# An RWKV-7 recurrence on one core: where a unit's first score pair stands, which queue carries three of its transfers, and when v is added

## The chip, the core and the metric

The kernel runs on one core of a Trainium2 chip. The core has a matrix engine (TensorE, "PE" in the profile), a vector engine (VectorE, "DVE"), a scalar engine (ScalarE, "ACT"), a general engine (GpSimd, "POOL") and a queue-only engine (SyncE, "SP"). Each has its own instruction stream, and they meet through semaphores. Sixteen DMA engines move data between DRAM and on-chip memory; here SyncE, ScalarE and GpSimd issue DMAs. An issue that waits for a semaphore holds up everything behind it on its engine. The metric is the device time of one execution in microseconds.

## The reference

One step of a trunk of two layers, for a prompt of 2048 tokens (with 16 learned tokens ahead of it) and for 8 samples of 4 tokens. Layer 0 is sliding-window attention. Layer 1 is RWKV-7 time mixing, with 16 heads of 64; its core, per token and head, is

```
sa = jnp.einsum('bhvk,bhk->bhv', S, a_t)
S = S * w_t[:, :, None, :] + sa[..., None] * b_t[:, :, None, :] + v_t[..., None] * k_t[:, :, None, :]
y_t = jnp.einsum('bhvk,bhk->bhv', S, r_t)
...
y = ((y - mean) * lax.rsqrt(var + GN_EPS)).reshape(B, T, R_WIDTH)
y = y * ln_g.astype(f32) + ln_b.astype(f32)
bonus = jnp.sum(r_h * k_h * r_k.astype(f32), axis=-1, keepdims=True) * v_h
y = (y + bonus.reshape(B, T, R_WIDTH)) * jax.nn.silu(g.astype(f32))
out = jnp.einsum('btw,wd->btd', y.astype(xn.dtype), w_out)
```

Then `out` is added to the residual, and a last RMS norm gives the result. The outputs are the normed rows, the attention windows, the last states S and the last rows of both layers' inputs.

## The kernel before

The program has three stages: attention (to about 600 us of the profiled span), the projections of the RWKV layer (to about 1600), and the recurrence (to the end). The change touches the third alone.

**Units and chunks.** The recurrence works on units of 128 tokens; unit 0 holds the learned tokens, units 1 to 16 the prompt, and the samples come last. A unit has four chunks of 32 tokens, counted from 0 here; where the text says third or fourth chunk, that is chunk 2 or 3. Within a chunk the per-token recurrence is replaced by matrix products: the 32 updates form a triangular system with one matrix per head. Its inverse depends on keys and decays alone, not on the state, and is prepared one or two units ahead. With it a chunk is this chain, in `chain` (line 1422) and `solve` (1394):

1. TensorE: `C<-Z,L`, the right-hand side from the state; ScalarE copies it to `R0s`. Z holds the state (64 rows) above the chunk's 32 rows of v and the 32 of the solution.
2. TensorE: `C<-R0s,TT`, the solve with the inverted triangles TT; ScalarE copies the result into Z (`Z<-C`, four copies).
3. TensorE: `C<-Z,LS`, the new state; VectorE scales it into the next chunk's Z (`Z<-C,pe`).

DMAs bring the rows of v for the next chunk into its Z (`Z<-v`, `new_Z`, `load_v`, lines 1359 to 1372), two a chunk. At the ends of chunks 1 and 3 (counted from 0) TensorE also makes the outputs `Y<-Z,L`.

**Work between the steps.** Other products of TensorE fill the time in which a chunk's chain waits for the other engines: the output projection of the unit before (`po<-wo,yp`), the gate (`pd<-wg,xg`, multiplied in by VectorE as `gt<-gt,pd`), transposes (`yps`), keys (`kt`), and the scores. A score pair is the scores of two chunks of the unit two ahead, `pz<-L,BK`, 64 matmuls in the profile (32 as the program writes them; `scores`, line 948). ScalarE copies the triangles out of them (`LAs<-pz`, four copies), VectorE masks the rest (`L<-pz,smk`, four products). BK and L come by DMA.

**The inverse** (`inverse`, line 976). When both pairs are there, LAs goes to DRAM (`la_d<-LAs`, two DMAs) and comes back with another layout (`LA<-la_d`, two DMAs). GpSimd scales it (`LA<-LA,ln`), then inverts by rows, in a chain of some 31 pairs `XT<-LA,X` and `X<-X,XT`, and scales the result (`X<-X,ln`). It goes to DRAM (`tt_d<-X`) and back as TT (`TT<-tt_d`), which the next unit's first solve needs. GpSimd also does small steps of two norms (`var`, `ms`) in the midst of that chain.

**After Y.** `group_norm` (1583) subtracts means, scales by `var`, by gamma (`lng`), adds beta (`lnb`), and at last v times the bonus (`ytm<-ytm,vt`, two products on VectorE). The gate multiplies it, TensorE transposes it, and `project_out` (1685) gives the residual's new rows, which leave by `out_y_prompt<-h`.

**What sets the order.** For units 2 to 14, `steady` (1766) writes the work out by hand, chunk by chunk, and `in_order()` (1753) fixes the order of VectorE, ScalarE and GpSimd as it is written; parts inside `released()` are free of that. TensorE's fillers are cut to budgets (`run(pe[ch], 1.2)`). The other units and SyncE's queue are ordered by a scheduler with priorities, so that a DMA's place on SyncE's queue can move when other things move. The helpers `mm`, `act`, `tt`, `stt` and `dma` record all operations on lines 38 to 50, so the profile's rows are told apart by their names.

In `steady`, `s` is the unit two ahead. Before the change the two score pairs are made in chunks 1 and 2, ahead of the solve, and `inverse(s)` begins in chunk 3:

```
if ch == 1:
    new_LAs(s)
if ch == 2:
    outputs(u, 1)
if ch in (1, 2):
    sc = scores(s, ch - 1)
    next(sc)
```

Of the kernel before, what the change touches and what calls it, by code (L numbers as in the profile page):

```python
# [30 lines left out]
def tile_hybrid_step(ctx: ExitStack, tc: tile.TileContext, a, o, c):  # L31
# [17 lines left out]
    def dma(out, in_, eng=None):  # L49
        return (eng or nc.sync).dma_start(out=out, in_=in_).ins  # L50
# [925 lines left out]
    def inverse(u, room=None, ln=None):  # L976

        nch = u.nch
        nl = nch * 16
        la_d = dramr.tile([2, nl // 2, 32, 32], F32, name="la_d", tag=f"la_d{nch}")  # L980
        u.tt_d = tt_d = dramr.tile([32, 4, 4 * nch * 32], F32, name="tt_d", tag=f"tt_d{nch}")
        for e in range(2):
            dma(la_d[e].rearrange("l j i -> j l i"),
                u.LAs[32 * e:32 * e + 32].rearrange("p h c g i -> p (h c g) i"), s_ if u.idx < PRE else None)
        eng = v_ if u.idx == 1 else g_
        if u.kind == "m":
            room = wl.tile([P, 2, 32 * 32], F32, name="roomm", tag="L", bufs=nbuf["L"])
        if room is not None:
            LA = room[:, 0].rearrange("p (j i) -> p j i", i=32)
            XX = room[:, 1].rearrange("p (a k i) -> p a k i", a=2, i=32)  # L990
        else:

            LA = wk.tile([P, 32, 32], F32, name="LA", tag="LA", bufs=2)
            XX = None
        if XX is None:
            X = wk.tile([P, 16, 32], F32, name="X", tag="X", bufs=2)
            XT = wk.tile([P, 16, 32], F32, name="XT", tag="XT")
        else:
            X, XT = XX[:, 0], XX[:, 1]
        if ln is None:  # L1000
            ln = wp.tile([P, 32], F32, name="ln", tag=("mu", "rst0")[u.idx % 2])
        if nch < 4:
            g_.memset(LA, 0.0)
            g_.memset(ln, 1.0)
        for hh in range(2):
            dma(LA[hh * 64:hh * 64 + nl], la_d.rearrange("e l j i -> (e l) j i"), s_ if u.idx < PRE else None)
            dma(ln[hh * 64:hh * 64 + nl], ln_d[u.idx].rearrange("q c g i -> (q c g) i"))
        tt(eng, LA, LA, ln.unsqueeze(2).broadcast_to([P, 32, 32]), ALU.mult)
        dma(X, c["laneid"])

        low = 16 if u.kind == "m" else 0

        part = {2: 16}.get(u.idx, 0)
        cut = [(v_, 0, part), (g_, part, 16)] if 0 < part < 16 else [(v_, 0, 16)] if part else [(eng, 0, 16)]
        for j in range(low, 31):
            if j in (8, 16, 22, 26):
                yield
            w = 3 - j % 4 if u.kind == "s" else 31 - j
            for eng, k0, k1 in cut if w else ():
                ks = slice(max(low // 2, k0), min(j // 2 + 1, k1))  # L1020
                shape = [P, ks.stop - ks.start, w]
                if shape[1] <= 0:
                    continue
                tt(eng, XT[:, ks, :w], LA[:, j:j + 1, j + 1:j + 1 + w].broadcast_to(shape), X[:, ks, j:j + 1].broadcast_to(shape), ALU.mult)
                tt(eng, X[:, ks, j + 1:j + 1 + w], X[:, ks, j + 1:j + 1 + w], XT[:, ks, :w], ALU.add)
        for eng, k0, k1 in reversed(cut):
            u.inverted = tt(eng, X[:, k0:k1], X[:, k0:k1], ln[:, None, :].broadcast_to([P, k1 - k0, 32]), ALU.mult)
        for hh in range(2):
            dma(tt_d[hh:32:2].rearrange("k q (l i) -> (q l) k i", i=32), X[hh * 64:hh * 64 + nl])
# [238 lines left out]
    with ExitStack() as ph:  # L1268
# [62 lines left out]
        def new_LAs(u):  # L1331
            u.LAs = wk.tile([64, 2, u.nch, 4, 32], F32, name="LAs", tag="LAs", bufs=1)
# [23 lines left out]
        anchors = {}  # L1356
        MARK = -1

        def new_Z(u, ch):

            Z = Zs[Zcount[0] % nbuf["Z"]]
            Zcount[0] += 1
            for e in range(2):
                load_v(u, ch, e, Z)
            return Z

        def load_v(u, ch, e, Z):
            b0, r0 = OS[e].start, u.off + ch * 32
            anchors["SP"] = dma(Z[b0 + 32:b0 + 64, e].rearrange("p g d -> p (g d)"), v_d[u.t][r0:r0 + 32, e, :])

        LScount = [0]
        over = []
# [32 lines left out]
        def released():  # L1405

            st = ExitStack()
            for x in anchors.values():
                st.enter_context(tc.issue_after(x))
            return st  # L1410
# [11 lines left out]
        def chain(u, ch):  # L1422
# [15 lines left out]
            anchors["PE"] = m  # L1438
            anchors["ACT"] = act(R0s, C[0][:, 0])

            if ch + 1 < u.nch:
                Zn = new_Z(u, ch + 1)
                u.Z.append(Zn)
            elif u.next is not None:
                Zn = new_Z(u.next, 0)
                u.next.Z.append(Zn)
            else:
                Zn = None
# [317 lines left out]
        def steady(i, u, pe):  # L1766
# [9 lines left out]
            for ch in range(4):  # L1776
# [4 lines left out]

                left = rests[::-1]
                del rests[:]
                with released():
                    if ch == 2:
                        next(inv.get(i + 1, idle()), None)
                for gen in left:
                    run(gen, to=MARK)
                with released():
                    for fn in side:  # L1790
                        fn()
                    del side[:]
                    if ch == 1:
                        new_LAs(s)
                    if ch == 2:
                        outputs(u, 1)
                    if ch in (1, 2):
                        sc = scores(s, ch - 1)
                        next(sc)
                    if ch == 3:  # L1800
                        kt = keys(u.next, 0)
                        next(kt)
# [4 lines left out]
                else:  # L1807
                    for gen in left:
                        run(gen)
                if ch in (1, 2):  # L1810
                    with released():
                        all_of(sc)
                run(pe[ch], 1.2)
                next(rec)
                with released():
                    if ch == 0:
                        kt = keys(u, 1) if i > 2 else idle()
                        next(kt, None)
                        first = L0s.pop(s.idx, None)
                        load_BK(s)  # L1820
                        s.L.append(first or load_L(s, 0))
                        all_of(kt)
                    if ch == 3:
                        all_of(kt)
                        inv[s.idx] = inverse(s)
                        next(inv[s.idx])
                    else:
                        next(inv.get(i + 1, idle()), None)
                if ch < 3:
                    run(norm, to=MARK)  # L1830
                else:
                    run(norms_[u.idx], to=MARK)
                run(pe[ch], 1.9)
                next(rec, None)
# [11 lines left out]
                run(pe[ch], to=MARK)  # L1846
                if ch == 0:
                    run(norm, to=MARK)
                rests.append(pe[ch])
                for part in PLAN.get((i, ch), ()):  # L1850
                    with released():
# [214 lines left out]
```

## Time and profile before

| what | value |
|---|---|
| time, median of 3 runs | 2562.52 us (2557.93 to 2570.88) |
| the profiled execution | 2564.59 us, its span 2562.7 us |
| mean granted TensorE clock | 0.945 |
| busy: TensorE, VectorE | 2245.7 us (88%), 1681.5 us (66%) |
| busy: ScalarE, GpSimd | 1168.8 us (46%), 1041.8 us (41%) |
| DMA | 312.99 MB, mean 122 GB/s |
| the recurrence's 13 hand-ordered units | from 1709.4 to 2359.1 us |

The page gives each engine's busy time, the chain that ended last, and groups of instructions with their idle time ahead. In a row of a timeline the numbers are the start and the length in microseconds, then engine, line, operation and tiles; brackets hold the idle time ahead and what ended it. "PE pz L38 <- DMA BK<-bk" in the waits means that TensorE's pz matmuls waited for that DMA. A DMA's row on SyncE ("SPq") shows its issue, not its transfer. In the chain of waits a DMA's row runs from the issue to the landing. The busy share of TensorE is an average over three stages; for this change only the rows from about 1640 us on matter.

### The profile page before, as it was taken

Reading aid. Unit: us, or ns where it says so; the run is one execution under the profiler, and the core shown is the slowest. Engines: PE = TensorE matmul, PEld = TensorE weight load, DVE = VectorE, ACT = ScalarE, POOL = GpSimd, SP = SyncE. Lnnn points to the kernel's source line nnn. Section 1 sums busy time; section 2 is a strip of 40 time slices with the busy share of each in tenths; the row PEclk is TensorE's granted clock in tenths of the full one; section 3 lists DMA queues with packets and bytes.
Section 4 is the critical chain, followed back from the end, with each engine's and each line's share of the span. In section 5 each row is a group of like instructions: output and inputs, shape, how many; then the busy total and the mean of one; then the engine's idle time right before and its main releaser. Section 6 shows DMA issues by size and latency. Waiting matters only on the chain.

```text
span 2562.7 us, 60891 instructions
## 1 busy us (share of the span) xinstructions
PE 2245.7 (88%) x24932; PEld 1544.6 (60%) x24932; DVE 1681.5 (66%) x3181; ACT 1168.8 (46%) x2799; POOL 1041.8 (41%) x1572
## 2 busy tenths in 40 slices
PE   6999999899999897899999998657887887888897
PEld 5877777777845445576677766344554554454553
DVE  7586674667747987766665556465666666666674
ACT  6676455566523344454444345233453444344432
POOL 4242122322111444433332333244667656666613
PEclk9999998999999998999999999768998999898998
DMA  8433222332447564322222225474555556455423
GB/s 205 124 108 111 68 67 79 132 99 74 139 114 234 198 232 147 121 84 103 78 93 89 92 86 164 102 219 110 137 135 130 122 135 144 103 137 131 106 62 74
DMA packets 346235, 312.99 MB, mean 122 GB/s; under 512 B 205546, under 2 KB 282218, under 8 KB 344131
## 3 DMA queue, kind: packets, MB, share of 16 engines
q1 hardware_dynamic: 337171, 296.71, 40.0%
q10 hardware_dynamic: 7168, 8.59, 1.6%
q0 software_dynamic: 1616, 3.79, 0.7%
q8 instruction: 196, 3.21, 0.5%
q14 instruction: 84, 0.69, 0.1%
HBM read 191.15 MB, written 119.84 MB: 121 GB/s over the span
## 4 chain that ended last, share of the span: by engine, by line
PE 33%; DVE 19%; DMA 17%; POOL 10%; ACT 9%; issue 8%; SPq 4%; ACTq 0%; POOLq 0%; DVEq 0%
PE pd L38 19%; PE po L38 5%; DVE xm L47 5%; SPq L50 4%; DMA BK<-bk 3%; DMA TT<-tt_d 3%; POOL X L44 3%; PE C L38 2%; DVE xpr L44 2%; POOL XT L44 2%; ACT ssb L41 2%; DMA wst<-in_rwkv_w_in 2%; DMA tt_d<-X 1%; PE pz L38 1%; DMA x<-in_x_prompt 1%
## 5 line engine op out<-in xcount | busy, mean ns | idle before, releaser
L38 PEld LDWEIGHTS <-yp 128*128 128x128 f16 x1488 | 143.2, 101 | 173.4 <-issue 25.7
L47 DVE SCALAR_TENSOR_TENSOR xm<-dx,mu,xn 128x256 f32<-128x256 f32 (+2 forms) x432 | 200.2, 522 | 48.1 <-POOL dx L44 47.3
L44 POOL TENSOR_TENSOR X<-X,XT 128x126 f32<-128x126 f32 (+24 forms) x458 | 196.9, 430 | 35.7
L38 PE MATMUL po<-wo,yp 128*128 128x512 f16 x768 | 201.5, 408 | 0.0
L38 PE MATMUL pd<-xp,wq 128*128 128x256 f16 (+2 forms) x1728 | 184.7, 265 | 12.3 <-DVE qp L47 9.0
L38 PE MATMUL pd<-wg,xg 128*128 128x512 f16 (+1 forms) x816 | 194.0, 385 | 0.5 <-issue 0.3
L44 POOL TENSOR_TENSOR XT<-LA,X 128x126 f32<-128x126 f32 (+24 forms) x458 | 175.8, 384 | 40.4 <-issue 6.7
L38 PE MATMUL pd<-wvv,xpr 128*128 128x512 f16 (+1 forms) x816 | 188.5, 388 | 0.0
L38 PE MATMUL pd<-xp,wg 128*128 128x256 f16 (+2 forms) x1728 | 186.6, 270 | 0.9 <-DVE xp L44 0.5
L38 PE MATMUL pd<-xpr,w 128*128 128x256 f16 (+2 forms) x1728 | 185.6, 267 | 0.0
L38 PE MATMUL pd<-xpr,wkk 128*128 128x256 f16 (+2 forms) x1728 | 179.5, 264 | 0.0
L38 PEld LDWEIGHTS <-wq 128*128 128x128 f16 x1728 | 158.5, 98 | 33.3 <-DVE qp L47 10.5
L44 POOL TENSOR_TENSOR ssb<-ssb,bias 128x512 f32<-128x512 f32 x64 | 86.3, 1355 | 222.8 <-DVE ssb L462 179.0
L38 PEld LDWEIGHTS <-wg 128*128 128x128 f16 x1728 | 161.4, 100 | 23.6 <-issue 4.0
L38 PEld LDWEIGHTS <-w 128*128 128x128 f16 x1728 | 157.3, 99 | 26.8 <-issue 9.7
L38 PEld LDWEIGHTS <-wkk 128*128 128x128 f16 x1728 | 158.2, 98 | 15.6 <-issue 0.4
L38 PE MATMUL pd<-w,yp 128*128 128x512 f16 x720 | 161.6, 382 | 4.2 <-DMA yp<-y 4.2
L44 POOL TENSOR_TENSOR ps<-wst,ps 128x1024 f16<-128x1024 f32 x32 | 69.5, 2171 | 221.8 <-ACT wst L41 203.7
L44 DVE TENSOR_TENSOR Z<-C,pe 64x256 f32<-64x256 f32 x256 | 108.0, 422 | 68.4 <-PE C L38 53.0
L38 PEld LDWEIGHTS <-xpr 128*128 128x128 f16 (+1 forms) x816 | 79.1, 100 | 102.1 <-issue 17.6
L44 DVE TENSOR_TENSOR xpr<-xm,xpr 128x512 f16<-128x512 f32 (+2 forms) x144 | 98.9, 708 | 55.2 <-ACT xpr L41 54.8
L41 ACT ACTIVATE ssb<-ssb,ng 128x128 f32<-128x128 f32 (+1 forms) x272 | 104.2, 384 | 57.0 <-DVE es L44 53.4
(357 smaller groups left out, 4699.1 us busy)
## 6 DMA issues: line engine op xcount, KB each, us to landing
wst<-in_rwkv_w_in SPq DMA_DIRECT2D x32, 512.0 KB
wsp<-ps SPq DMA_DIRECT2D x32, 512.0 KB
BK<-bk SPq DMA_DIRECT2D x32, 512.0 KB
x<-in_x_prompt SPq DMA_DIRECT2D x29, 512.0 KB
xn<-xn SPq DMA_DIRECT2D x14, 1028.0 KB
ar<-aro SPq DMA_DIRECT2D x28, 512.0 KB
bk<-bko SPq DMA_DIRECT2D x28, 512.0 KB
L<-ar SPq DMA_DIRECT2D x38, 256.0 KB
```

The costliest lines, as they stand in the source:

```text
L38: return t_.matmul(out=out, lhsT=lhsT, rhs=rhs, start=start, stop=stop, **kw).ins
L41: return s_.activation(out=out, in_=in_, func=func, **kw).ins
L44: return e.tensor_tensor(out=out, in0=in0, in1=in1, op=op).ins
L47: v_.scalar_tensor_tensor(out=out, in0=in0, scalar=scalar, in1=in1, op0=op0, op1=op1)
L50: return (eng or nc.sync).dma_start(out=out, in_=in_).ins
```

## The change

Four things change in the recurrence, for the hand-ordered units.

- **Scores.** The first pair of the unit two ahead is made at the end of chunk 1, behind that chunk's state update, no longer at its head. The second stays in chunk 2.
- **Triangles' way out.** `la_d<-LAs` is issued by ScalarE (before: SyncE, but for the first units), in chunk 2, directly behind the copies that fill LAs. The function `inverse` gets a `yield` there, so that the loads back, `LA<-la_d`, are still placed in chunk 3.
- **Rows of v.** For all but the first and last units the `Z<-v` loads are issued by ScalarE, behind its copy to `R0s`.
- **v added.** The last part of the group norm, `ytm<-ytm,vt`, runs at the head of chunk 3, no longer in chunk 2.

The diff, without hunk lines:

```diff
 def inverse(u, room=None, ln=None):
...
             dma(la_d[e].rearrange("l j i -> j l i"),
-                u.LAs[32 * e:32 * e + 32].rearrange("p h c g i -> p (h c g) i"), s_ if u.idx < PRE else None)
+                u.LAs[32 * e:32 * e + 32].rearrange("p h c g i -> p (h c g) i"), s_)
+        yield
         eng = v_ if u.idx == 1 else g_
...
-        def new_Z(u, ch):
+        def new_Z(u, ch, eng=None):
...
-                load_v(u, ch, e, Z)
+                load_v(u, ch, e, Z, eng)
...
-        def load_v(u, ch, e, Z):
+        def load_v(u, ch, e, Z, eng=None):
             b0, r0 = OS[e].start, u.off + ch * 32
-            anchors["SP"] = dma(Z[b0 + 32:b0 + 64, e].rearrange("p g d -> p (g d)"), v_d[u.t][r0:r0 + 32, e, :])
+            x = dma(Z[b0 + 32:b0 + 64, e].rearrange("p g d -> p (g d)"), v_d[u.t][r0:r0 + 32, e, :], eng)
+            if eng is None:
+                anchors["SP"] = x
...
             anchors["ACT"] = act(R0s, C[0][:, 0])

+            eng = s_ if 1 < u.idx < len(us) - 2 else None
             if ch + 1 < u.nch:
-                Zn = new_Z(u, ch + 1)
+                Zn = new_Z(u, ch + 1, eng)
                 u.Z.append(Zn)
             elif u.next is not None:
-                Zn = new_Z(u.next, 0)
+                Zn = new_Z(u.next, 0, eng)
...
         def steady(i, u, pe):
...
                 left = rests[::-1]
                 del rests[:]
+                if ch == 3:
+                    run(norm)
                 with released():
                     if ch == 2:
                         next(inv.get(i + 1, idle()), None)
...
-                    if ch == 1:
-                        new_LAs(s)
                     if ch == 2:
                         outputs(u, 1)
-                    if ch in (1, 2):
-                        sc = scores(s, ch - 1)
+                        sc = scores(s, 1)
                         next(sc)
...
-                if ch in (1, 2):
+                if ch == 2:
                     with released():
+                        inv[s.idx] = inverse(s)
+                        next(inv[s.idx])
                         all_of(sc)
                 run(pe[ch], 1.2)
                 next(rec)
...
                     if ch == 3:
                         all_of(kt)
-                        inv[s.idx] = inverse(s)
                         next(inv[s.idx])
...
-                if ch < 3:
+                if ch < 2:
                     run(norm, to=MARK)
-                else:
+                elif ch == 3:
                     run(norms_[u.idx], to=MARK)
...
                 if ch == 0:
                     run(norm, to=MARK)
+                if ch == 1:
+                    with released():
+                        new_LAs(s)
+                        all_of(scores(s, 0))
                 rests.append(pe[ch])
```

The diff shows little of what happens to the queues. Three places do.

First SyncE's queue, in a unit in the middle of the recurrence (v_110 and the like are buffers of one block), from one `out_y_prompt` toward the next. Before:

```order
L50 DMA xg<-xg_130 128x16x128
L50 DMA BK<-bk_150 128x4x256 x2
...
L50 DMA ln<-ln_192 64x32 x2
L50 DMA X<-c_laneid 128x512
L50 DMA Z_19046<-v_111 32x512
L50 DMA la_d<-LAs 32x32x32 x2
L50 DMA L<-ar_159 64x1024
L50 DMA tt_d<-X 64x16x32 x2
L50 DMA LA<-la_d 64x1024
L50 DMA vt<-v_110 128x512 x2
L50 DMA LA<-la_d 64x1024
L50 DMA TT<-tt_d 64x1x512 x2
```

and now:

```order
L50 DMA xg<-xg_130 128x16x128
L50 DMA BK<-bk_150 128x4x256 x2
L50 DMA bont<-bo_211 128x16
L50 DMA L<-ar_159 64x1024 x2
L50 DMA tt_d<-X 64x16x32 x2
L50 DMA ln<-ln_193 64x32 x2
L50 DMA LA<-la_d 64x1024 x2
L50 DMA TT<-tt_d 64x1x512 x2
L50 DMA X<-c_laneid 128x512
L50 DMA vt<-v_110 128x512 x2
L50 DMA out_y_prompt<-h_25545 128x1024
```

la_d and the rows of v are gone from it, vt stands behind TT and no longer between the two LA, and ln and X<-c_laneid, which belong to a later inverse, stand behind tt_d.

Second, ScalarE from the state copy of chunk 1 to that of chunk 2 in the same part of the program. Before:

```order
L41 ACTIVATE R0s<-C 128x256
L41 ACTIVATE po,ssq_24848<-h_24847 128x512
L41 ACTIVATE LAs<-pz 32x2x128 x4
L41 ACTIVATE Z_19046<-C 32x256 x4
...
L41 ACTIVATE LAs<-pz 32x2x128 x4
L41 ACTIVATE Z_19047<-C 32x256 x4
```

and now:

```order
L41 ACTIVATE R0s<-C 128x256
L50 DMA Z_19047<-v_109 32x512 x2
L41 ACTIVATE po,ssq_24848<-h_24847 128x512
L41 ACTIVATE Z_19046<-C 32x256 x4
L41 ACTIVATE LAs<-pz 32x2x128 x4
...
L50 DMA Z_19044<-v_109 32x512 x2
...
L41 ACTIVATE LAs<-pz 32x2x128 x4
L50 DMA la_d<-LAs 32x32x32 x2
L41 ACTIVATE Z_19047<-C 32x256 x4
```

The first LAs copies moved behind chunk 1's Z copies; the rows of v and la_d are new, la_d ahead of chunk 2's Z copies. On TensorE, in chunk 2, the second score pair stood ahead of the whole solve and now stands in its middle, behind VectorE's masks of the first pair:

```order
L38 MATMUL C<-R0s,TT 32x64 x8
L38 MATMUL pz<-L,BK 64x64 x32
L38 MATMUL C<-R0s,TT 32x64 x8
```

Third, SyncE's queue at the start of the recurrence, where the blocks of the output weights (wo) are loaded; the tt_d and TT shown are those of unit 2, the first of the hand-ordered ones. Before:

```order
L50 DMA wo_20144<-wsp_225 128x2048
L50 DMA wo_20146<-wsp_226 128x2048
L50 DMA tt_d<-X 64x16x32 x2
L50 DMA TT<-tt_d 64x1x512 x2
```

and now:

```order
L50 DMA wo_20144<-wsp_225 128x2048
L50 DMA wo_20146<-wsp_226 128x2048
L50 DMA wo_20255<-wsp_227 128x2048
L50 DMA wo_20257<-wsp_228 128x2048
L50 DMA xg<-xg_126 128x16x128
L50 DMA tt_d<-X 64x16x32 x2
L50 DMA wo_20437<-wsp_229 128x2048
L50 DMA wo_20439<-wsp_230 128x2048
...
L50 DMA wo_20590<-wsp_232 128x2048
L50 DMA h_20659<-h_1_84 128x1024
...
L50 DMA TT<-tt_d 64x1x512 x2
```

All eight blocks of wo, and a residual's rows, now stand ahead of that TT on the queue; before, six of them stood behind it.

## The prediction, made before the changed kernel ran

> **What bounds the kernel now.** I first read which waits stop TensorE in the nine units from 1860 to 2311 us, where each unit of 128 tokens repeats the last (us in total, times, longest):
>
> ```profile
> PE pz L38 <- DMA BK<-bk: 42.0, 13, 5.5
> PE C L38 <- DMA TT<-tt_d: 13.3, 10, 2.2
> PE C L38 <- issue: 11.9, 8, 1.5
> ```
>
> The large wait, 4.7 us a unit, is on BK, the operand of the score matmuls. It would be easy to stop here and credit the change with it. But TT, GpSimd's inverted triangles, is waited for in every unit as well, so TensorE would only reach the next TT sooner. I therefore read GpSimd's groups over the same stretch, and its timeline around one inverse:
>
> ```profile
> L44 POOL TENSOR_TENSOR LA<-LA,ln 128x1024 f32<-128x1024 f32 x10 | 19.1, 1915 | 104.6 <-DMA LA<-la_d 63.9 <-DMA bont<-bo 20.7 <-DMA out_y_prompt<-h 10.9
> ```
> ```profile
> 1765.56 0.56 POOL L44 TENSOR_TENSOR XT<-LA,X 128x31 f32<-128x31 f32 x1
> ...
> 2161.13 0.24 POOL L44 TENSOR_TENSOR XT<-LA,X 128x31 f32<-128x31 f32 x1
> ...
> 2197.46 1.65 POOL L44 TENSOR_TENSOR X<-X,ln 128x512 f32<-128x512 f32 x1
> 2209.72 1.92 POOL L44 TENSOR_TENSOR LA<-LA,ln 128x1024 f32<-128x1024 f32 x1 [10.62 <-DMA bont<-bo]
> 2211.72 0.24 POOL L44 TENSOR_TENSOR XT<-LA,X 128x31 f32<-128x31 f32 x1
> ...
> 2312.62 0.56 POOL L44 TENSOR_TENSOR XT<-LA,X 128x31 f32<-128x31 f32 x1
> ```
>
> GpSimd stands idle 10.46 us (104.6 over 10) ahead of every inverse and is otherwise in its chain of XT and X products. The first and last XT rows shown are 547.06 us and 11 inverses apart: 49.73 us each. One inverse, from 2161.13 to the end of its last product at 2199.11, is 38.0 us; then come 12.6 us to the next XT. A period is that inverse plus that gap. GpSimd sets the pace as well as TensorE, and the question is what fills the gap. The rows of SyncE's queue answer it:
>
> ```profile
> 2197.83 0.97 SPq L50 DMA_DIRECT2D la_d<-LAs  x2
> 2198.86 0.63 SPq L50 DMA_DIRECT2D L<-ar  x1
> 2199.57 1.34 SPq L50 DMA_DIRECT2D tt_d<-X  x2
> 2201.02 1.06 SPq L50 DMA_DIRECT2D LA<-la_d  x1
> 2202.18 1.02 SPq L50 DMA_DIRECT2D vt<-v  x2
> 2203.25 0.48 SPq L50 DMA_DIRECT2D LA<-la_d  x1
> 2203.82 1.10 SPq L50 DMA_DIRECT2D TT<-tt_d  x2
> ...
> 2207.34 0.38 SPq L50 DMA_DIRECT2D out_y_prompt<-h  x1
> ```
>
> The inverse ends at 2199.11. The scores go out to DRAM (la_d) only 1.3 us before that, the second half of LA is issued at 2203.25 behind 512 KB of vt, and its consumer starts 6.0 us after that issue ends. TT is last.
>
> **The change part by part.** The period is worked out for two loops; the slower one counts.
>
> GpSimd's loop. la_d now leaves ScalarE's queue in the third chunk, so it has landed before the inverse under way ends. vt goes behind TT. What follows the end of an inverse on SyncE is tt_d twice, ln twice, LA twice. Prices:
>
> ```profile
> 2194.26 1.11 SPq L50 DMA_DIRECT2D ln<-ln  x2
> ...
> 1686.31 1.10 SPq L50 DMA_DIRECT2D LA<-la_d  x2
> ```
> ```profile
> 1691.14 1.91 POOL L44 TENSOR_TENSOR LA<-LA,ln 128x1024 f32<-128x1024 f32 x1 [21.06 <-DMA LA<-la_d]
> ```
>
> 1.34 + 1.11 + 1.10 and 0.2 between them put the end of LA's issue at 3.75 us (today 4.6: 2203.73 against 2199.11). In the early inverse at 1686, with no vt between, the consumer came 3.73 us after the issue ended (1687.41 to 1691.14). So GpSimd starts again at 7.5 us instead of 10.6, and its XT comes 2.0 us later, at 9.5. The period becomes 37.1 + 9.5 = 46.6 us (37.1 is the mean inverse, 49.73 less a gap of 12.6), 3.1 less. Bounds: if the other loads on the 16 DMA engines (tt_d and ln here, TT right behind) hold LA back to the 6.0 us of today, only the issue gain of 0.9 is left; if LA lands as fast as 3 us after its issue, the period is 46.
>
> [...]
>
> TensorE's loop. Its rows in the unit from 2160.6 to 2211.4 (50.8 us):
>
> ```profile
> 2163.03 0.64 PE L38 MATMUL C<-R0s,TT 32*32 32x64 f32 x28 [1.47 <-DMA TT<-tt_d]
> ...
> 2178.43 1.25 PE L38 MATMUL pz<-L,BK 64*64 64x64 f32 x32 [4.48 <-DMA BK<-bk]
> 2180.64 1.14 PE L38 MATMUL pz<-L,BK 64*64 64x64 f32 x32 [0.96 <-DMA BK<-bk]
> 2181.71 2.74 PE L38 MATMUL po<-wo,yp 128*128 128x512 f16 x6
> 2184.38 1.08 PE L38 MATMUL C<-R0s,TT 32*32 32x64 f32 x32
> ...
> 2194.94 0.65 PE L38 MATMUL C<-R0s,TT 32*32 32x64 f32 x32
> ...
> 2201.51 0.65 PE L38 MATMUL C<-Z,L 128*32 128x64 f32 x32 [0.74 <-PE pd L38]
> ...
> 2215.55 1.46 PE L38 MATMUL po<-wo,yp 128*128 128x512 f16 x6
> ```
>
> Behind the BK stall the same six po take 2.74 instead of 1.46, the solve 1.08 instead of 0.65: 1.7 us more, a slow clock besides the 5.44 of waiting. Three rows of the chain around the next unit's head price what surrounds it:
>
> ```profile
> 2200.26 3.50 DMA tt_d<-X
> ...
> 2204.41 10.04 DMA TT<-tt_d
> ...
> 2221.56 10.98 DMA BK<-bk
> ```
>
> BK lands at 2232.54, 33.4 us after the inverse's end; the four issues of v rows ahead of it (a half microsecond each, as la_d's row has it) go from SyncE, which makes 31.4. The scores were due some 5 us before it landed, at 28; they now stand some 7 us of TensorE work later, and TT comes about 2 us earlier: due at 33. So BK is some 1.5 us ahead of need and the stall with its slow clock goes; the out_y, h and xg transfers that BK queues behind must not grow by more than that, or the rest returns as a wait. Taken off also: 1.47 (TT, counted anew below) and 0.74 (state update behind the v adds). New costs, by VectorE's and ScalarE's rows:
>
> ```profile
> 2194.46 2.80 DVE L44 TENSOR_TENSOR L<-pz,smk 64x512 f32<-64x512 f32 x4 [1.55 <-ACT LAs L41]
> 2197.28 2.37 DVE L44 TENSOR_TENSOR ytm<-ytm,vt 128x512 f32<-128x512 f32 x2
> ```
> ```profile
> 2193.66 1.55 ACT L41 ACTIVATE LAs<-pz 32x256 f32<-32x256 f32 x4 [0.92 <-PE pz L38]
> ```
>
> The v adds now stand ahead of the gate product of the fourth chunk, whose transposes are next on TensorE: +2.4. The second pair's matmuls need the banks that the first pair's masks read (2.80 us), and its LAs copies with both la_d issues (1.0 us, as SyncE's row shows) stand ahead of the Z copies that TensorE waits for: between 0 and 4, taken at 1.4, since 9 matmuls of the gate cover the rest. The 8 issues of v rows cost ScalarE some 4 us a unit at the same half microsecond:
>
> ```profile
> 2160.60:2211.40 50.80, 41.59 (x768) 24.89 (x761) 32.21 (x51) 21.18 (x54) 32.84 (x70) 0.90 0.53 126
> ```
>
> The fourth busy time is ScalarE's, 21.18 of 50.80, so its idle time hides them, except in the fourth chunk: there the issue waits until tt_d has let go of a semaphore that both use, 4.65 us after an inverse's end (2203.76 against 2199.11). With the Z copies (1.6 us) behind it TensorE has them at 6.5 or so; it gets to them some 8.5 us into the chunk, behind 15 gate matmuls and the v adds, and the chunk begins 1 to 2 us ahead of the inverse's end. Nothing, just; without that cover up to 4 us. Sum: 50.8 − 5.44 − 1.7 − 1.47 − 0.74 + 2.4 + 1.4 = 45.3 us.
>
> So GpSimd's 46.6 counts, and TensorE waits some 1.3 us a unit for TT, as now. 11 periods × 3.1 = 34 us.
>
> The start of the recurrence. The inverse for unit 4 (the first XT row above) began late today:
>
> ```profile
> 1748.92 1.14 SPq L50 DMA_DIRECT2D la_d<-LAs  x2
> ```
> ```profile
> 1708.11 7.47 DMA TT<-tt_d
> ...
> 1782.43 8.51 issue
> ```
>
> la_d sat in SyncE's queue behind weights, and LA behind la_d; POOL's late variance held the state update, and TensorE stood 8.51 us. With la_d from ScalarE I put that XT near 1758.6, 7 us earlier. Against it: the loads of wo are hoisted ahead of TT of unit 2, the first hand-ordered one, which today lands at 1715.6 (1708.11 and 7.47). The page's slices move at most
>
> ```profile
> GB/s 205 124 108 111 68 67 79 132 99 74 139 114 234 198 232 147 121 84 103 78 93 89 92 86 164 102 219 110 137 135 130 122 135 144 103 137 131 106 62 74
> ```
>
> 234 GB/s. Eight blocks, xg and a residual are 5 MB, 21 us at that rate, begun at about 1697; with TT's own 7.5 it lands near 1725, 10 us later. It delays TensorE's unit 2, while GpSimd's next inverse does not yet wait for it. Taken −7, between −9 and +8. Stages one and two keep their order, and the tail keeps its rows and shifts whole, give or take 5 us.
>
> Total: 34 + 7 = 41 us off the profiled 2564.6 us (span 2562.7 and 1.9 around it), so 2523.5; the median shown is 2.1 below that run, which makes 2521 us.
>
> **Rivals.**
>
> Both loops give more (chance 0.12): LA lands 3 us after its issue and TensorE waits nowhere new. At 45.3 us a period, 11 × 4.4 = 48, and 9 at the start: 2505. For it: TensorE's own sum; against it: TT still moves the same way, 10 us after its issue.
>
> One wait replaces another (0.20): ScalarE's blocked issue in the fourth chunk, or LA slowed by TT beside it, eats half. 48.2 a period: 11 × 1.5 = 17, start −4: 2541. For it: three of the moved transfers meet within 5 us of an inverse's end on the same engines.
>
> Issue time alone (0.10): LA's transfer is as slow as today, because TT, tt_d and ln share its engines, and only its issue ends 0.9 us earlier: 11 × 0.9 = 10, nothing at the start: 2552. BK's stall turns into a longer wait for TT. For it: TT keeps 10 us from issue to use with nothing of this change in its way; against it: the 3.73 us of the early inverse. [...]
>
> Slower (0.08): ScalarE's queue becomes the bound. The v row's issue waits for tt_d, and behind it stand yp's and Z's copies, so C<-Z,LS of the fourth chunk starts over 4 us later each unit, and la_d adds 1 us to each third chunk. It decides once the new costs pass 8.2 us instead of 3.8 (45.3 + 4.4 = 49.7); with 5.8 us more it is 51.1: 11 × 1.4 = +15, and +8 at the start: 2586.
>
> **How the numbers follow.** The forecast, 2521, has 0.50. A measurement of this kernel tells about 0.5% from no change, 12.8 us: from 2550 to 2575. Faster takes the forecast, the first and the second rival, less a little for their upper ends: 0.80. Same takes the third and that rest: 0.12. Slower: 0.08. The forecast's own range, 2508 to 2534, comes from 46 to 47.5 a period and the start's bounds. For 8 in 10 it is widened to the first two rivals: 2503 to 2550.
>
> **What would show it.** Right: BK gone from TensorE's waits, po x6 at 1.5 us throughout; GpSimd's idle time ahead of LA 7 to 8 us and XT to XT 46 to 47; LA's two issues adjacent; unit 4's XT near 1759; a wait for TT of 1 to 3 us a unit. Wrong: idle ahead of LA still 10 us, TensorE waiting on ScalarE's Z in the fourth or third chunk for over 3 us, or unit 2 starting later by more than 10 us without the later ones catching up.

## The result, and the profile after

The changed kernel takes 2523.07 us (median of 4 runs, 2521.12 to 2526.93) against 2566.70 us before (4 runs on the same chips, 2557.93 to 2571.59): a ratio of 0.9836, 95% interval 0.9802 to 0.9869. The forecast was 2521. Profile against profile the gain is 37.7 us (2564.59 to 2526.93; span 2562.7 to 2525.2).

TensorE's waits from 1840 to 2290 us, some ten units:

```profile
PE C L38 <- DMA TT<-tt_d: 21.3, 12, 3.3
PE yps L1676 <- DVE gt L44: 11.5, 10, 1.2
PE C L38 <- ACT Z L41: 8.2, 12, 1.3
```

BK is gone from them. TT is now the largest, 2.2 us a unit, and the two waits that the change was to bring, on the gate product behind the v adds and on ScalarE's Z copies, are there with 1.2 and 0.9 us a unit. GpSimd's timeline, with the first and last XT rows that answer to those shown of before:

```profile
1763.71 0.24 POOL L44 TENSOR_TENSOR XT<-LA,X 128x31 f32<-128x31 f32 x1
...
2171.52 1.27 POOL L44 TENSOR_TENSOR X<-X,ln 128x512 f32<-128x512 f32 x1
2181.86 1.91 POOL L44 TENSOR_TENSOR LA<-LA,ln 128x1024 f32<-128x1024 f32 x1 [9.07 <-DMA Z<-v]
2183.85 0.24 POOL L44 TENSOR_TENSOR XT<-LA,X 128x31 f32<-128x31 f32 x1
...
2276.21 0.24 POOL L44 TENSOR_TENSOR XT<-LA,X 128x31 f32<-128x31 f32 x1
```

The eleven periods now take 512.50 us, 46.59 each, against 49.73: 34.6 us, nearly the whole gain. The inverse ends at 2172.79 and the next XT comes 11.06 us later (12.6 before). SyncE's queue in that gap:

```profile
2172.82 1.34 SPq L50 DMA_DIRECT2D tt_d<-X  x2
2174.21 1.33 SPq L50 DMA_DIRECT2D ln<-ln  x2
2175.65 2.37 SPq L50 DMA_DIRECT2D LA<-la_d  x2
2178.12 1.10 SPq L50 DMA_DIRECT2D TT<-tt_d  x2
2179.26 0.43 SPq L50 DMA_DIRECT2D X<-c_laneid  x1
2179.79 1.18 SPq L50 DMA_DIRECT2D vt<-v  x2
```

LA is issued adjacent and ahead of vt, as forecast, but its issue ends 5.2 us after the inverse, not 3.75 (4.0 to 5.2, 4.7 on the mean of the eleven inverses from 1800 to 2266 us), and its consumer starts 3.8 us after that (3.85 on the mean). GpSimd's row names Z<-v as what ended the wait, but the load that it waits for is LA: its second half lands at 2181.70 in the trace, 0.16 us ahead of the product, and the distance is the same, within 0.01 us, in all eleven.

The period also fell inside the inverse. GpSimd's groups, before (1860 to 2311 us) and after (1840 to 2290 us):

```profile
L44 POOL TENSOR_TENSOR X<-X,XT 128x126 f32<-128x126 f32 (+22 forms) x279 | 120.5, 432 | 21.9
L1704 POOL TENSOR_SCALAR ms<-ssq 128x2 f32<-128x2 f32 x9 | 1.7, 194 | 11.0 <-ACT po L41 10.6
```
```profile
L44 POOL TENSOR_TENSOR X<-X,XT 128x126 f32<-128x126 f32 (+22 forms) x299 | 121.2, 405 | 23.4
L44 POOL TENSOR_TENSOR LA<-LA,ln 128x1024 f32<-128x1024 f32 x10 | 19.1, 1912 | 86.0 <-DMA Z<-v 77.2 <-DMA LA<-la_d 8.8
L1708 POOL TENSOR_SCALAR ms<-ssq 128x2 f32<-128x2 f32 x10 | 3.6, 362 | 1.3 <-ACT po L41 0.5
```

Idle time ahead of LA went from 10.46 to 8.60 us. Inside the inverse, GpSimd's wait for the second output projection's sum (1.2 us an inverse, the ms row) is nearly gone; that TensorE no longer stands in chunk 1 is the likely reason. It makes up most of the 1.2 us by which the inverse got shorter: over units 5 to 13 the idle time in it fell from 1.2 to 0.2 us. The X products take 27 ns less each in these rows, but the XT products and the ms steps take more, so that the work itself changed by only some 0.2 us.

### The profile page after: what moved, and what is told of

It is laid out like the page before. It is cut to its first block, busy times and chain, and to the rows that moved or that the text cites. A ratio compares the mean times of both kernels' runs of the same rounds, so it can differ in the third digit from the quotient of the medians.

```text
span 2525.2 us, 60868 instructions
## 1 busy us (share of the span) xinstructions
PE 2238.5 (89%) x24932; PEld 1539.7 (61%) x24932; DVE 1666.3 (66%) x3181; ACT 1169.9 (46%) x2799; POOL 1035.9 (41%) x1572
## 5 line engine op out<-in xcount | busy, mean ns | idle before, releaser
L47 DVE SCALAR_TENSOR_TENSOR xm<-dx,mu,xn 128x256 f32<-128x256 f32 (+2 forms) x432 | 199.6, 521 | 48.4 <-POOL dx L44 47.1
L44 POOL TENSOR_TENSOR X<-X,XT 128x126 f32<-128x126 f32 (+24 forms) x458 | 186.1, 406 | 35.7
L38 PE MATMUL po<-wo,yp 128*128 128x512 f16 x768 | 191.3, 392 | 0.0
```

The source lines that it names most:

```text
L38: return t_.matmul(out=out, lhsT=lhsT, rhs=rhs, start=start, stop=stop, **kw).ins
L44: return e.tensor_tensor(out=out, in0=in0, in1=in1, op=op).ins
L47: v_.scalar_tensor_tensor(out=out, in0=in0, scalar=scalar, in1=in1, op0=op0, op1=op1)
```

## The experiments

Each was compared with the kernel before on the same chip; the ratio is to before. For the table, the period is the time from unit 5's first XT to unit 13's, over 8; the gap is from the end of an inverse's last product to the next XT; the inverse is the rest. These three come from one profiled execution of each kernel, and that can lie anywhere among its runs: the slowest of four for the changed kernel and of six without the scores' move, the fastest of four without the v rows' move. Unit 4's first XT lies between 1762.9 and 1774.0 us in them, so some microseconds of a difference in time arise before the loop.

| kernel | period | gap | inverse | time, us | ratio (95%) |
|---|---|---|---|---|---|
| before | 49.8 | 12.5 | 37.3 | 2566.7 | 1 |
| changed | 46.7 | 10.6 | 36.1 | 2523.1 | 0.9836 (0.9802 to 0.9869) |
| scores only | 53.7 | 16.7 | 37.0 | 2613.1 | 1.0182 (1.0148 to 1.0215) |
| queues only | 54.0 | 16.8 | 37.1 | 2614.8 | 1.0191 (1.0155 to 1.0227) |
| without the v adds' move | 54.5 | 17.5 | 37.0 | 2623.2 | 1.0227 (1.0196 to 1.0257) |
| without the scores' move | 49.5 | 8.9 | 40.6 | 2550.4 | 0.9929 (0.9906 to 0.9953) |
| without the v rows' move | 44.7 | 8.8 | 35.9 | 2509.1 | 0.9785 (0.9760 to 0.9809) |
| without la_d's move | 45.5 | 9.7 | 35.7 | 2520.2 | 0.9830 (0.9809 to 0.9851) |
| GpSimd longer | 50.2 | 10.1 | 40.1 | 2566.5 | 0.9991 (0.9977 to 1.0005) |
| TensorE longer | 46.2 | 10.5 | 35.8 | 2536.2 | 0.9883 (0.9857 to 0.9908) |
| LA earlier, first | 46.0 | 10.1 | 35.9 | 2532.3 | 0.9870 (0.9838 to 0.9902) |
| LA earlier, second | 46.2 | 6.2 | 39.9 | 2520.8 | 0.9810 (0.9787 to 0.9832) |
| LA earlier, third | 47.1 | 10.2 | 36.9 | 2538.9 | 0.9907 (0.9879 to 0.9935) |
| the start | 46.6 | 10.7 | 35.9 | 2526.0 | 0.9835 (0.9807 to 0.9863) |

### Scores only

```diff
 # the kernel before, with:
+                if ch == 1:
+                    with released():
+                        new_LAs(s)
+                        all_of(scores(s, 0))
```

> The kernel before with only the first score pair moved to the end of chunk 1; la_d, the rows of v and the v adds as before. Theory (GpSimd's loop of inverse and gap sets the pace): BK goes from TensorE's waits, but GpSimd's idle time ahead of LA stays at 10 us or more and the inverses stay 49 to 51 us apart, so the time is within 10 us of before (2555 to 2575); what TensorE saved on BK comes back as a wait for TT of 5 us or more a unit. Rival (TensorE's wait for BK was the bound): 5 to 7 us a unit are gained, 2480 to 2510.

It is slower than before by 1.8%. BK is gone from TensorE's waits, so the rival (BK was the bound) is refuted: nothing came of it. But the theory's "within 10 us" missed too, and SyncE's queue shows why; behind it GpSimd's row:

```profile
2184.28 1.44 SPq L50 DMA_DIRECT2D LA<-la_d  x1
2185.81 1.01 SPq L50 DMA_DIRECT2D vt<-v  x2
2187.20 1.11 SPq L50 DMA_DIRECT2D TT<-tt_d  x2
2188.36 0.50 SPq L50 DMA_DIRECT2D LA<-la_d  x1
```
```profile
2196.93 1.91 POOL L44 TENSOR_TENSOR LA<-LA,ln 128x1024 f32<-128x1024 f32 x1 [14.87 <-DMA LA<-la_d]
```

The scheduler put LA's second half behind TT as well. GpSimd's gap grew from 12.5 to 16.7 us, and the period with it. TensorE's wait for TT came to 3.3 us a unit (23.8 us from 1900 to 2290), less than the 5 that the theory gave; another 43.3 us of its waits there have no cause that the profile names.

### The queues only

la_d and the rows of v on ScalarE; scores and v adds as before.

```diff
 # the changed kernel, with:
-                if ch == 1:
-                    with released():
-                        new_LAs(s)
-                        all_of(scores(s, 0))
-                if ch == 3:
-                    run(norm)
 # and both at their old places
```

> The changed kernel with the first score pair back at the head of chunk 1 and the v adds back in chunk 2, so only la_d and the rows of v on ScalarE's queue are left of the change. vt then stands ahead of LA on SyncE's queue. Theory: la_d is early, but vt's 512 KB ahead of LA keep GpSimd idle for 10 to 12 us, and TensorE waits for BK 3 us or more a unit: period 48 to 50 us, 2545 to 2570. Rival (spreading issues over two queues is the gain): 46 to 47 us a period, 2515 to 2530.

Slower than before by 1.9%, which is worse than either side expected. The gap is 16.8 us; here, too, TT stands ahead of LA's second half in every inverse. So neither the queues nor the scores alone bring any of the gain; by themselves both cost.

### Without the v adds' move

```diff
 # the changed kernel, with:
-                if ch == 3:
-                    run(norm)
-                if ch < 2:
+                if ch < 3:
                     run(norm, to=MARK)
```

> The changed kernel with only the v adds back in chunk 2. That lets vt's load be issued ahead of LA again, 512 KB more in front of it, at 1.0 us of issue time. Theory (bytes ahead of LA delay it): GpSimd's idle time ahead of LA rises from 8.6 to 10.5 to 12 us, period 48.5 to 50, 2540 to 2560. [...] Second rival (the v adds in chunk 3 cost TensorE more than they save): 2505 to 2518, as the 1.15 us wait ahead of the yps transposes goes.

The smallest edit costs the most: 4% against the changed kernel. vt's tile is free once the v adds have read it. With the adds in chunk 2 the load is ready before the inverse ends, and on SyncE's queue it stands ahead of LA:

```profile
2184.11 1.01 SPq L50 DMA_DIRECT2D vt<-v  x2
2185.22 0.48 SPq L50 DMA_DIRECT2D LA<-la_d  x1
2185.85 1.11 SPq L50 DMA_DIRECT2D TT<-tt_d  x2
2187.01 0.49 SPq L50 DMA_DIRECT2D LA<-la_d  x1
```
```profile
2197.30 1.92 POOL L44 TENSOR_TENSOR LA<-LA,ln 128x1024 f32<-128x1024 f32 x1 [16.69 <-DMA LA<-la_d]
```

LA's second half is issued by 2187.50 and its consumer starts 9.8 us later, against 3.8 in the changed kernel. Issue time explains 1.0 us of vt's and 1.1 of TT's on the queue; the other 6 come after LA's issue. They are not vt's alone: vt has landed by 2187.7, LA's second half at 2197.24. TT is what was issued between these two besides LA's first half, and the transfers are slow there: from 2193.0 to 2195.5 the DMA engines are busy for 0.13 of their time and move 51 GB/s, against 0.86 and 252 from 2184.7 to 2187.7. That TT is what holds LA's second half up is the author's reading of these rows. The other kernels agree with it. From the end of LA's issue to its consumer it takes 3.5 to 4.0 us on the mean in the kernels of the table that issue LA on SyncE with neither vt nor TT just ahead of its second half, 6.0 in the kernel before, with vt, and 8.4 to 9.3 in the three kernels with vt and TT (scores only, queues only, and this one). No run put TT there without vt.

What stands ahead of LA cost more here than its issue: GpSimd's idle time ahead of LA is 16.69 us in this unit and 9.07 in the changed kernel's, and of the 7.62 us between them 1.65 lie ahead of the end of LA's issue and 5.97 behind it. The size was underestimated: 12 us was the upper end for the idle time, and it was 15 to 17.

### Without the scores' move

```diff
 # the changed kernel, with scores(s, 0) back at the head of chunk 1:
+                    if ch == 1:
+                        new_LAs(s)
-                        sc = scores(s, 1)
+                    if ch in (1, 2):
+                        sc = scores(s, ch - 1)
```

> The changed kernel with only the first score pair back at the head of chunk 1. In the changed kernel's trace BK lands 0.3 us before its use at the end of chunk 1; at the head it is due 6 to 7 us earlier. Theory (both loops are near each other, so either can become the bound): TensorE waits 5 to 6 us a unit for BK and runs some 2 us at a slow clock, 50 to 53 us a unit, 2565 to 2600. Rival (GpSimd alone sets the pace, BK's wait only eats TensorE's slack): 46 to 48 us a unit, 2520 to 2540.

A piece of its chain of waits, then TensorE's timeline:

```profile
2175.47 11.23 DMA BK<-bk
```
```profile
2185.11 1.13 PE L38 MATMUL pz<-L,BK 64*64 64x64 f32 x32 [5.43 <-issue]
2186.74 1.14 PE L38 MATMUL pz<-L,BK 64*64 64x64 f32 x32 [0.50 <-DMA BK<-bk]
2187.81 2.74 PE L38 MATMUL po<-wo,yp 128*128 128x512 f16 x6
```

The stall is back (the first half of BK lands at 2185.0, so the row's "issue" is BK too), and the six po behind it take 2.74 us, against 1.46 at 2215.55 in the kernel before. The gap is short, 8.9 us, but GpSimd now waits inside the inverse, 40.6 us, for the output projection's sum (46.9 us in eight inverses from 1860 to 2250): TensorE leads. 49.5 us a period is just under the theory's 50 to 53 and over the rival's 46 to 48. The time, 2550.4 us, lies between the theory's 2565 to 2600 and the rival's 2520 to 2540; the profiled execution took 2562.9, so the period of the others was probably a little shorter. With GpSimd's gap shortened, moving the scores is worth 27 us; in the kernel before, the same move cost 46, with TT ahead of LA's second half.

### GpSimd longer, TensorE longer

```diff
 # the changed kernel: seven XT products of units 5 to 14 done twice
+                for _ in range(2 if 4 < u.idx < 15 and 9 < j < 17 else 1):
                     tt(eng, XT[:, ks, :w], ...)
 # the changed kernel: the gate's transposes of units 3 to 13 done three times
+            for _ in range(3 if 2 < u.idx < 14 else 1):
                 for j in range(4):
                     t_.transpose(out=yps[:, j, :], ...)
```

> The changed kernel with seven of the XT products of each inverse of units 5 to 14 done twice, 3.0 to 3.4 us more of GpSimd in ten inverses. Theory (GpSimd's loop is the bound): the period rises by the same 3.0 to 3.4 us, the time by 28 to 34 us, 2550 to 2557. Rival (TensorE is the bound and GpSimd has slack): TensorE's wait for TT grows and takes it up, less than 1.2 us a unit, 2523 to 2535.

> The changed kernel with the four gate transposes of units 3 to 13 made three times over, the same values again, 2.4 us more of TensorE in each of eleven units. Theory (GpSimd's loop is the bound, TensorE has the 2 us in which it waits for TT to spare): TensorE's wait for TT shrinks from 2.1 us to under 0.8, the time rises by 0 to 9 us, 2523 to 2532. Rival (TensorE is the bound): the whole 26 us come on top, 2545 to 2552.

On GpSimd the seven products and what they cost around them made the inverse 4.0 us longer, more than the 3.0 to 3.4 that had been reckoned. The gap shrank by 0.5, so the period rose by 3.5. The time rose by 43 us (the spans by 40.0), above the theory's range; 37 of the spans' 40 stand between unit 4's first XT and unit 15's, and unit 4's came 4.1 us later. On TensorE the eight extra transposes cost 0.87 us twice a unit, less than the 2.4 reckoned:

```profile
2144.47 1.53 PE L1677 MATMUL yps<-ident,gt 128*128 128x128 f32 x12
2145.83 1.46 PE L38 MATMUL po<-wo,yp 128*128 128x512 f16 x6
```

The period did not rise (46.2 against 46.7). TensorE's waits for TT fell from 21.3 to 11.5 us over the same 450 us. The time rose by 13 us all the same, 4 over the theory's range and 9 under the rival's. In the profile, whose span grew by 9.0, unit 4's first XT came 6.9 us later and unit 16's only 0.4, so the loop took that back; the other 8.6 come behind it, and their cause stays open. So GpSimd's loop is the bound in the changed kernel, and TensorE has at least these 1.7 us a unit to spare.

### Without la_d's move, without the v rows' move

```diff
 # la_d back on SyncE
-                u.LAs[...], s_)
+                u.LAs[...], s_ if u.idx < PRE else None)
 # rows of v back on SyncE
-            eng = s_ if 1 < u.idx < len(us) - 2 else None
+            eng = None
```

> The changed kernel with only la_d back on SyncE's queue, where it now stands ahead of tt_d with nothing of la_d's own unit before it. Theory (what keeps GpSimd waiting is the order tt_d, ln, LA, vt, not which queue issues la_d): la_d still lands before the inverse under way ends, the period stays at 46 to 47 us, 2518 to 2528. Rival (la_d on ScalarE is what opens the gap): GpSimd idle 10 us or more ahead of LA, 2540 or more.

> The changed kernel with only the rows of v back on SyncE's queue. Their issues stand ahead of BK again (some 1.8 us), and BK lands only 0.3 us before its use in the changed kernel; ln, on the other hand, is no longer issued between tt_d and LA. Theory: TensorE waits for BK 1.5 to 3.5 us at the end of chunk 1, while GpSimd's idle time ahead of LA falls by about 1 us; TensorE becomes the bound at 47.5 to 49 us a unit, 2530 to 2545. Rival (which queue issues the rows of v does not matter): 2518 to 2527.

la_d's queue does not matter for the time: 2520.2, as the theory had it. The period even fell to 45.5, under the theory's 46 to 47, and TensorE's waits for ScalarE's Z copies, which no longer stand behind la_d's issue, from 7.0 to 0.8 us (1860 to 2250 us); in this profile unit 4's first XT came 5.3 us later. The rows of v matter, and the other way than either expected: this kernel is the fastest of all, 2509.1 us, with BK not waited for. So neither of the two moves to ScalarE's queue was needed for the gain. No run took both back at once. SyncE's queue, then ScalarE's:

```profile
2146.92 1.13 SPq L50 DMA_DIRECT2D ln<-ln  x2
2148.10 0.58 SPq L50 DMA_DIRECT2D X<-c_laneid  x1
...
2156.64 1.35 SPq L50 DMA_DIRECT2D tt_d<-X  x2
2158.09 1.28 SPq L50 DMA_DIRECT2D LA<-la_d  x2
2160.06 1.10 SPq L50 DMA_DIRECT2D TT<-tt_d  x2
2161.21 0.90 SPq L50 DMA_DIRECT2D vt<-v  x2
2162.16 0.43 SPq L50 DMA_DIRECT2D out_y_prompt<-h  x1
```
```profile
2149.47 2.08 ACTq L50 DMA_DIRECT2D la_d<-LAs  x2
2151.59 1.56 ACT L41 ACTIVATE Z<-C 32x256 f32<-32x256 f32 x4 [2.15 <-DMA X<-c_laneid]
```

With the v rows on SyncE, ln and X<-c_laneid are issued in chunk 2, ahead of the inverse's end, as they were before the change. LA's issue then ends 2.8 us after the inverse and not 5.2, out_y goes out 5.5 us after it and not 9.0, and BK behind it is early. The gap is 8.8 us and TensorE, at 44.7 us a unit, waits for TT 0.5 us. It is 14 us faster than the changed kernel by the medians; the two ratios' intervals (0.9760 to 0.9809 and 0.9802 to 0.9869) just overlap, though its slowest run, 2514.6, is under the changed kernel's fastest, 2521.1. The periods, 44.7 against 46.7, show in which loop the difference lies: 1.8 of the 2 us are in the gap. That ln and X<-c_laneid in the gap are the reason is read from the queue; no run moved these two alone.

### LA earlier

```diff
 # the changed kernel: LA's two loads on ScalarE, too; first at the end of chunk 2,
 # then (second kernel) between its Z copies and the gate's copy
-            dma(LA[...], la_d..., s_ if u.idx < PRE else None)
+            dma(LA[...], la_d..., s_ if u.idx < PRE or 3 < u.idx < len(us) - 1 else None)
...
+        yield
...
+                        next(inv[s.idx])
 # third kernel: the second, with the v adds back in chunk 2
```

> The changed kernel with the two LA loads also on ScalarE's queue, at the end of chunk 2 behind its copies, so LA no longer waits for the end of the inverse under way. Theory: GpSimd's idle time ahead of LA falls from 8.6 us to under 3 us and TensorE becomes the bound at 44 to 45.5 us a unit with no wait for TT, 2490 to 2510. Rival (TensorE or ScalarE's queue is the bound already): the units stay at 46 to 47 us, 2518 to 2528.

> As la_early, but the LA loads stand between ScalarE's Z copies and the gate's copy of chunk 2, where they share their semaphore with an old load of L and no longer with tt_d. Theory: they are issued as soon as la_d has landed and hold up nothing; GpSimd's idle time ahead of LA falls under 6 us, TensorE has no wait for TT and none for R0s, units take 43.5 to 45 us: 2485 to 2505. Rival (the waits in la_early came from ScalarE having too much to issue, not from the shared semaphore): TensorE still waits for R0s over 1 us a unit, 2515 or more.

> As la_early2, with the v adds back in chunk 2. vt's load then stands ahead of TT on SyncE, but not ahead of LA, which ScalarE issues. Theory (in la_early2 TensorE is the bound, and 2 us of each unit are its wait for the gate product behind the v adds): that wait goes, TT has slack enough for vt ahead of it, 43 to 44.5 us a unit, 2500 to 2513. Rival (vt ahead of TT makes TT late): TensorE waits for TT 2 us or more a unit, 2520 or more.

None came near its hope. The first takes 2532.3 us, the second 2520.8 (2518.5 to 2522.5), the third 2538.9. The first's loop is no slower than the changed kernel's, 46.0 us a period; in its profile unit 4's first XT came 10.2 us later, at 1774.0. ScalarE in the first and in the third:

```profile
2136.08 1.10 ACTq L50 DMA_DIRECT2D LA<-la_d  x2
2137.22 0.38 ACT L41 ACTIVATE R0s<-C 128x256 f32<-128x256 f32 x1 [2.18 <-issue]
```
```profile
2133.19 5.87 ACTq L50 DMA_DIRECT2D LA<-la_d  x2
2139.11 0.60 ACT L41 ACTIVATE gt<-pd 128x512 f32<-128x512 f32 x1 [6.38 <-DMA tt_d<-X]
```

Eight semaphores serve the DMAs of this loop in turn: in the changed kernel's trace each is used 50 or 51 times from 1700 to 2300 us, none of these 403 issues is followed by the next on its semaphore before its transfer has landed, and 57 times the next one begins within 0.1 us of that landing. In the first and the third, LA shared one with tt_d, so it could not be early, and ScalarE's copies stood behind it: in the traces tt_d landed at 2135.93 and 2138.59, and the LA issues that share with it begin at 2136.08 and 2138.61. In the second, LA shares with an old load of L, TensorE no longer waits for R0s (21.8 us in the first and 24.6 in the third, from 1860 to 2250), the gap falls to 6.2 us, and another thing appears. VectorE's row beside GpSimd's:

```profile
2132.52 2.28 DVE L44 TENSOR_TENSOR gt<-gt,ytm 128x512 f32<-128x512 f32 x1
```
```profile
2132.34 1.91 POOL L44 TENSOR_TENSOR LA<-LA,ln 128x1024 f32<-128x1024 f32 x1 [3.85 <-DMA LA<-la_d]
```

The gate product takes 2.28 us where it begins 0.18 us after GpSimd's large product, 0.69 at 2177.17, where it begins 0.07 us before it, and TensorE waits for it up to 2.9 us. TensorE's chain leads there: GpSimd's inverse, 3 us of waits within it included, is 39.9 us.

### The start

```diff
 # the changed kernel
-                    with released():
+                    with released(), tc.issue_after(us[2].landing):
                         load_w(...)
...
```

> The changed kernel with the loads of wo held behind the load of TT of unit 2. Theory: TT of unit 2 lands near 1715 us, not near 1733; unit 2 ends 8 to 12 us sooner, la_d and LA of unit 4 follow, its first XT comes 8 to 14 us sooner than 1763.7, and the time falls by 8 to 14 us to 2509 to 2516. Rival (unit 4's inverse waits for something else at the start, its own predecessor or the traffic of the wo loads): first XT within 3 us of 1763.7, 2520 to 2526.

2526.0 us, no gain, as the rival had it. TT of unit 2, which lands at 1725.8 in the changed kernel, did go ahead of the wo loads, issued at 1710.7 and not 1715.6, and TensorE's long wait fell from 10.5 to 4.0 us. Unit 4's first XT came at 1762.9 against 1763.7. What it waits for is this (the changed kernel, ScalarE and SyncE):

```profile
1746.16 3.21 ACTq L50 DMA_DIRECT2D la_d<-LAs  x2
```
```profile
1757.27 1.08 SPq L50 DMA_DIRECT2D LA<-la_d  x2
```

la_d's second half is held until 1749 by a semaphore that TT uses, and lands 8 us after its issue; it takes 2.5 in the later units. In both kernels LA is issued at 1756 or 1757. Whether the wo loads' traffic or something else slows la_d there was not separated.

## Why the prediction was right, and where it was not

**GpSimd's loop sets the pace.** Right, and shown: 4.0 us more in GpSimd's inverse lengthened the period by 3.5, 1.7 us more on TensorE did not show in it. Where TensorE led (without the scores' move, and in the second kernel with LA earlier), the inverse was stretched from inside by waits, to 40.6 and 39.9 us. TensorE's own loop, put at 45.3 us, can't be read in the changed kernel; without the v rows' move the period is 44.7.

**The period, 46.6 us.** Measured 46.59, by two errors that cancel, so that the exact hit is luck. The gap was put at 9.5 and was 10.6 on the mean. The landing was priced well (3.73 us, measured 3.85); the end of LA's issue was not, 3.75 against 4.7. The issues of ln and LA in the gap, put at 1.11 and 1.10 us, took up to 2.4 each. What stretched them is open: in the unit shown, the transfers that LA's first issue waits for had landed by 2170.93, long before it. The inverse was put at 37.1 and was 36.1: GpSimd was taken to be in its chain all the time outside the gap, but it waited inside the inverse for TensorE's late projection, 1.2 us. The step that failed is the assumption that an inverse lasts as long as before.

**vt behind TT.** Right as a row, but the forecast took it as given. It is the v adds' move that brings it; it was costed only as a loss of 2.4 us for TensorE, and is worth 100 us against the same kernel without it, since there TT, too, comes ahead of LA's second half.

**The v adds, +2.4 us.** Mis-sized: they cost TensorE 1.15. The row explains it:

```profile
2174.66 1.28 DVE L44 TENSOR_TENSOR ytm<-ytm,vt 128x512 f32<-128x512 f32 x2
```

1.28 us instead of 2.37: they now fall into GpSimd's gap, beside none of its products.

**BK 1.5 us ahead.** It was 0.3: the second half landed at 2160.1 and the scores began at 2160.40. Right in sign, with next to no margin.

**ScalarE's queue costs nothing.** Right for the wait in chunk 3, which blocked ScalarE until 2178.4 with no wait of TensorE behind it. Wrong for the whole: with the v rows there, ln and X<-c_laneid are issued in the gap, and taking the rows back gained 14 us by the medians.

**The start, −7 us.** Wrong. Unit 4's first XT came 1.9 us earlier. That TT of unit 2 would be late was right (its second half landed at 1725.8, as the 1725 forecast, and TensorE waited 10.5 us for the first), and it did not matter. la_d was issued from ScalarE early enough, but the price of its way out was taken from the quiet units.

**The sum.** 34.6 + 1.9 + 1.0 of the tail is the 37.5 of the spans, against 41 forecast.

## What to carry to other kernels

Where two engines' loops are within a few microseconds of each other, undoing one part of a change tells little about the part: here the scores' move alone and the two queue moves alone lose 2% each, and together with the v adds' move they gain 1.6%. Read what stands between the end of one round and the start of the next on the queue that the loop passes through, and follow every move of an operation to the loads that wait for its buffers, since these change their place in the queue without a line of the diff naming them. After a change, compare the loop's parts and not only its period, and look for what came into the gap that need not be there.

## What the runs showed of the hardware that had not been expected

TensorE's slow clock came behind short waits, too. Behind a wait for TT of 2.16 us in the changed kernel:

```profile
2141.21 0.64 PE L38 MATMUL C<-R0s,TT 32*32 32x64 f32 x28 [2.16 <-DMA TT<-tt_d]
...
2142.59 2.77 PE L38 MATMUL po<-wo,yp 128*128 128x512 f16 x6
```

The six po take 2.77 us, not 1.46, at a granted clock of 0.50 from 2142.59 to 2145.36 (1.00 from 2145.8 to 2170). It is not regular. Of the ten units with such waits from 1840 to 2290 us, six had po at over 2 us behind them, with 1.9 to 4.4 us of waiting in the unit; four did not, with 0.3, 1.3, 1.8 and 2.4 us. Before the change (1860 to 2311 us) it was two of nine, with 2.0 and 3.0 us; the other seven waited 0.3 to 2.1. The longest single wait for TT in these units is 3.33 us; what decides was not shown.

VectorE's gate product and v adds took longer where one of GpSimd's large products was under way: the gate product 2.28 us instead of 0.69 (the second kernel with LA earlier), the v adds 2.37 (before) instead of 1.28 (changed). No run put them side by side on purpose, but the fourteen traces hold 646 of these products of 128x512 between 1800 and 2350 us. The 357 with no work of GpSimd beside them all took 0.68 or 0.69 us. 31 took over 1.0 (10 of the 44 in the kernel before, none of the 48 in the changed one), and each of these began after one of GpSimd's two large products (LA<-LA,ln or X<-X,ln) had begun and ended 0.54 or 0.55 us after that product did. Of the 22 that began before GpSimd's product, 20 took 0.69 us. An estimate from 0.69 and 0.55: such a product ends as one would that began 0.14 us before the end of GpSimd's. Why was not shown.
